# Summing the modulation vectors over partitions: two plain float32 matmuls into partitions 0 and 32 instead of four split ones

## The chip, the cores and the metric

The kernel runs on one core of a Trainium2 chip. The metric is the device time of one execution in microseconds (us). Before the change it is 2858.25 us, the median of three runs (2858.05 to 2859.9).

## The reference

The program computes one inference step through two trunk layers for 640 tokens (128 context, 512 latent) of width 1024. What matters here is the modulation at the head of each layer:

```python
mod_ctx = jax.nn.silu(c_ctx)[None, :] @ w_mod[l] + b_mod[l]
mod_lat = jax.nn.silu(c) @ w_mod[l] + b_mod[l]
...
sh1, sc1, g1, sh2, sc2, g2 = jnp.split(mod[:, None, :], 6, axis=-1)
```

`w_mod[l]` is 1024 x 6144, so each layer makes two vectors (one for each of two conditioning vectors) of 6144 numbers. The rest of a layer is projections, attention, a bidirectional state-space scan, two convolutions and a feed-forward block, nearly all of it matrix products over the 640 tokens.

## The kernel before, in words

Every operation is first recorded (by the helper at line 178, which is why nearly every row of the profile has L178), then a list scheduler (`Flow.issue`) orders all operations of the five lanes (TensorE, ScalarE, VectorE, GpSimd and the DMA queue of SyncE) by modelled costs and issues them in that order. Where several operations of a lane are ready, a rank decides, by the class of the operation: on TensorE the modulation class "m" goes first and the main stream "f" last; on ScalarE and VectorE "m" goes last. Buffers are granted in the order in which they were asked for. The cost model takes 4 cycles a column at 2.4 GHz for a plain float32 matmul and one cycle a column for a float32r one.

The big products run as float32r matmuls: each operand is split in two parts, `hi` (a rounding cast on ScalarE) and `lo` (the rest, a subtraction on VectorE), and three matmuls make one product. A few small products (scan states, cumulative sums) are plain float32 matmuls. In the names of the rows, `pf` is the PSUM of the main stream, `p`, `pp` and `pq` that of the others, `wh` and `wl` are the two parts of the weights.

The modulation is computed in groups of 512 columns, `mod_gen(l, m)`. The first four groups of layer 0 take another path (`mod_T_first`). The other 20 go through `mod_gen`: groups 4 to 9 of layer 0 step by step between the operations of attention (class "d", buffer `mw`), and groups 10 and 11 of layer 0 and all twelve of layer 1 in the feed-forward stage of layer 0 (class "m"). In each, VectorE multiplies eight pieces of `w_mod` (128 rows each) by the column of silu(cond) that belongs to them and adds them up in two accumulators `acc[0]` and `acc[1]` (named `macc` in the rows, 128 x 512, one for each conditioning vector). What is left is a sum over the 128 partitions, and that is done on TensorE: both accumulators are split in `hi` and `lo`, and four float32r matmuls with a stationary tile `pick[:, cnd, :]` (128 x 2: one column of ones, one of zeros) accumulate into rows 0 and 1 of one PSUM tile. `mod_rows` adds the bias (two copies of the same row, loaded by one DMA) and stores both rows in `modrow` in DRAM by one DMA. `mod_T` and `gate_bc` read `modrow` later.

Of the kernel before, what the change touches and what calls it, by code (L numbers as in the profile page):

```python
# [18 lines left out]
P = 128  # L19
# [21 lines left out]
def _mask(dims, cache={}):  # L41
    """Bits of the free elements that an access pattern touches."""
    m = cache.get(dims)
    if m is None:
        m = 1
        for s, n in reversed(dims):
            if s == 0 or n == 1:
                continue
            if m == 1 and s == 1:
                m = (1 << n) - 1  # L50
            else:
                b = 0
                for i in range(n):
                    b |= m << (s * i)
                m = b
        cache[dims] = m
    return m
# [22 lines left out]
class Flow:  # L80
    """Records the program as operations on tiles, orders them with a list scheduler (dependences by the
    elements touched, buffers granted in the order in which they were asked for) and issues them in that order."""

# [258 lines left out]
def hybrid_step_kernel(  # L342
# [42 lines left out]
    def keep(shape, dt, tag):  # L385
        return flow.tile(kp, shape, dt, tag, nm(tag), 1)
# [20 lines left out]

# [1 line left out]
    cst = keep([P, 3 * P], F32, "cst")  # L409
# [5 lines left out]
    dve.memset(neghalf, -0.5)  # L415
    pick = keep([P, 2, 2], F32R, "pick")

    def emit_consts():
        maskf = t2((P, P))
        dma.dma_start(cst[:, P:3 * P], consts[:, P:3 * P])  # L420
        dma.dma_start(maskf, consts[:, 3 * P:4 * P])
        dve.tensor_copy(mask, maskf)
        dve.memset(pick.rearrange("p a b -> p (a b)").bitcast(F32), 0.0)
        for k in range(2):
            act.copy(pick[:, k, k:k + 1], ones[:, 0:1])

# [1 line left out]
    cT = keep([P, 2, 8], F32, "cT")  # L428
# [13 lines left out]

# [1 line left out]
    modrow, attn_s, x_s, bm_s, row_s, sz_s, tg_s, ga_s, pb_s, y_sc = [], [], [], [], [], [], [], [], [], []  # L444
# [12 lines left out]

# [1 line left out]
    def wraw(parts, wide):  # L459
# [41 lines left out]

    # token-major product: stationary tokens, moving weights of 512 columns
    def tok_major(units, xT, ks):
# [14 lines left out]

    # tokens in two parts: tiles 0 to 2 and tiles 3 and 4
    def part(i):  # L520
# [5 lines left out]

    # tokens that wait in DRAM: two quads of feature tiles, in pieces of four, tile after tile
    def tok_load(src, q0):
# [17 lines left out]

    # feature-major product: stationary weights of 128 columns, moving tokens
    def feat_half(unit, cw, o, hT, b):
# [23 lines left out]
    def norm_x(xh, xns, junk):  # L572
        """Both halves of a token tile over their root mean square."""
        ssp = sm(2)
        for n in range(2):
            act.activation(junk, xh[n], AF.Square, accum_out=ssp[:, n:n + 1])
        ss = sm(1)
        pool.tensor_add(ss, ssp[:, 0:1], ssp[:, 1:2])
        rstd_of(ss, 1, 1.0 / DM)
        for n in range(2):  # L580
            dve.tensor_scalar(xns[n], xh[n], ss, None, ALU.mult)
# [20 lines left out]
    def norm_tile(x0, x1, t, i, modT, hT):  # L602
        """x0 and t are written over."""
        xns = [x0, t]
        norm_x([x0, x1], xns, t)
        for n in range(2):
            h = xns[n].rearrange("p (k t) -> p k t", k=4)
            norm_mod(norm_T(xns[n]), h, i, n, modT, hT, n == 0)

# [1 line left out]
    def mod_rows(l, m, ps, br):  # L611
        dve.tensor_add(br[0:2, :], ps[0:2, :], br[0:2, :])
        dma.dma_start(modrow[l][:, m * 512:(m + 1) * 512], br[0:2, :])

    def mw():
        """Of its own while attention holds the other buffers."""
        return t2() if flow.cls == "m" else flow.tile(tmp, [P, 512], F32, "mw", nm("mw"), 1)

    def mod_bias(l, m):
        br = mw()  # L620
        dma.dma_start(br[0:2, :], bc(b_mod[l:l + 1, m * 512:(m + 1) * 512], [2, 512]))
        return br

    def mod_gen(l, m):
        acc = [flow.tile(tmp, [P, 512], F32, "macc", nm("macc"), 2) for _ in range(2)]
        for kt in range(8):
            w = mw()
            dma.dma_start(w, w_mod[l, kt * P:(kt + 1) * P, m * 512:(m + 1) * 512])
            for cnd in range(2):
                s = cT[:, cnd, kt:kt + 1]  # L630
                if kt == 0:
                    dve.tensor_scalar(acc[cnd], w, s, None, ALU.mult)
                else:
                    dve.scalar_tensor_tensor(acc[cnd], w, s, acc[cnd], ALU.mult, ALU.add)
            yield
        ps = ps1()
        for cnd in range(2):
            hi, lo = t2(dt=F32R), t2(dt=F32R)
            split(hi, lo, acc[cnd])
            mm(ps[0:2, :], pick[:, cnd, :], hi, cnd == 0, False)  # L640
            mm(ps[0:2, :], pick[:, cnd, :], lo, False, cnd == 1)
        mod_rows(l, m, ps, mod_bias(l, m))
        yield
# [7 lines left out]

    # the first shifts and scales, straight to features on partitions: columns of silu(cond) in two parts
    def mod_T_first(ws):
# [3 lines left out]
        for n in range(2):  # L657
            for m in range(2):
                us = ws[4 * n + 2 * m:4 * n + 2 * m + 2]
                ps = psf()  # L660
                for kt in range(8):
                    for r in range(2):
                        w = us[kt // 4][r][:, (kt % 4) * 512:(kt % 4) * 512 + 512]
                        mm(ps[0:4, :], cs[:, kt].rearrange("p r a -> p (r a)"), w, kt + r == 0, kt + r == 8)
                flow.cls = "d"
                rows = t2() if n else flow.tile(tmp, [P, 512], F32, "macc", nm("macc"), 2)
                flow.cls = "f"
                o = m * 1024 + n * 512
                dma.dma_start(rows[4:6, :], bc(b_mod[0:1, o:o + 512], [2, 512]))
                act.copy(rows[0:4, :], ps[0:4, :])  # L670
                pt = flow.tile(p1, [P, 512], F32, "p1", nm("p1"), 2)
                for k in range(4):
                    pe.transpose(pt[:, 6 * k:6 * k + 6], rows[0:6, k * P:(k + 1) * P], ident[0:6, 0:6])
                # the two parts and the bias
                tv = t[:, :, 8 * m + 4 * n:8 * m + 4 * n + 4]
                dve.tensor_reduce(tv, pt[:, 0:24].rearrange("p (k r a) -> p a k r", k=4, r=3), AX.X, ALU.add)
                if m == 1:
                    dve.tensor_scalar(tv, tv, 1.0, None, ALU.add)
            yield t
# [23 lines left out]

# [1 line left out]
    def conv_bufs():  # L705
# [21 lines left out]
    def later(fn):  # L727
        """Record what was put off last, put this off in its stead."""
        old = list(pending)
        pending[:] = [fn]  # L730
        for f in old:
            f()
# [6 lines left out]

    # ================= the program as a list of items =================  # L740
    items = []
# [58 lines left out]
    def layer(l):  # L800
# [13 lines left out]
        def qk_normed(ps, n0, nh, t, a):  # L814
            """RMS norm per head, then rotary (t >= 1) or plain weights (t == 0); token-major."""
            src = ps[:, n0:n0 + nh * P]
# [83 lines left out]
        def attn_gen(g):  # L900
            kT, V = S["kT"], S["V"]
            qT, qc = S["qT", g], S["qc", g]
            # context tokens
            s = ps1()
# [53 lines left out]

# [1 line left out]
        def dt_item(ws):  # L960
# [71 lines left out]

# [1 line left out]
        def to_tok(cc, dst):  # L1034
            """feature-major padded [128, 642] -> token-major [128 tok, 5, 128 feat]"""
            for c0, n in ((0, 3), (3, 2)):
# [44 lines left out]

# [1 line left out]
        def z_item(g):  # L1083
# [21 lines left out]

# [1 line left out]
        def ssd_gen(g):  # L1107
# [19 lines left out]
            for c in range(NT):  # L1127
                o = col(c)
                dst = pb[:, 0:P] if c == 0 else pa[:, (c - 1) * P:c * P]
                mm(dst, Bf[:, o:o + P], Cf[:, o:o + P], True, True)  # L1130
            # C over B, and B by tokens behind it, in two parts
            s = slice(0, COLS)
# [21 lines left out]

            # context states leave as they are
            x = x_chunk(0)
# [227 lines left out]

# [1 line left out]
        def run_gen(key, make, n):  # L1386
# [127 lines left out]

# [1 line left out]
    AHEAD = 2  # L1516
# [68 lines left out]
```

## Time and profile before

| | |
|---|---|
| median of three runs | 2858.25 us |
| span of the profiled execution | 2854.8 us, 41191 instructions |
| own time of the profiled execution | not listed apart; the three runs lie 3.25 to 5.1 us above its span |
| TensorE (PE) busy | 2816.5 us, 99%, 15620 matmul records |
| VectorE (DVE) busy | 2066.4 us, 72% |
| ScalarE (ACT) busy | 1291.9 us, 45% |
| GpSimd (POOL) busy | 90.5 us, 3% |
| granted TensorE clock | 0.998 of 2.4 GHz |
| DMA | 478.45 MB, mean 168 GB/s |

A busy share is that of an engine over the whole span. A matmul record lasts from its issue to the end of its results, longer than the time that it holds the array: in a stream, the distance from one start to the next is what a matmul costs. `PEld` is the load of the stationary tile, which mostly runs under the matmul before it.

### The profile page before, as it was taken

To read this page: it belongs to the slowest core of one execution; us is meant where nothing else is said; L and a number is where in the kernel's file an instruction comes from. 1 tells how busy PE (TensorE), PEld (TensorE's weight loads), DVE (VectorE), ACT (ScalarE), POOL (GpSimd) and SP (SyncE) were. 2 spreads that over 40 slices of the span, in tenths; PEclk is the share of its full clock that TensorE was granted. 3 is DMA by queue.
4 is the path that set the end of the run, shared out by engine and by line. 5 is a ranking of instruction groups with operands and counts; after the bars stand their busy time and mean duration, and the time that the engine had idled before them with its cause. 6 is when DMAs were issued, how large, how long until landed. Compare 5 with 4: busy or idle time off the path is not lost.

```text
span 2854.8 us, 41191 instructions
## 1 busy us (share of the span) xinstructions
PE 2816.5 (99%) x15620; PEld 2456.6 (86%) x15620; DVE 2066.4 (72%) x2851; ACT 1291.9 (45%) x2255; POOL 90.5 (3%) x408
## 2 busy tenths in 40 slices
PE   6999999999999999999999999999999999999999
PEld 4898997877788898998979989887887888989898
DVE  7878775987799599997677666598779456545554
ACT  6454654445353453452444645544454325524342
POOL 1200000000000000000011000000000000000000
PEclk9999999999999999999999999999999999999999
DMA  7343444677868546455352223457667553252423
GB/s 262 100 125 126 126 151 143 225 247 245 275 219 275 180 136 215 167 175 180 98 168 85 94 95 100 155 199 251 220 235 258 203 175 132 86 166 65 155 84 111
DMA packets 309679, 478.45 MB, mean 168 GB/s; under 512 B 19808, under 2 KB 139792, under 8 KB 304360
## 3 DMA queue, kind: packets, MB, share of 16 engines
q1 hardware_dynamic: 309480, 475.81, 50.0%
q8 instruction: 123, 2.02, 0.3%
q14 instruction: 76, 0.62, 0.1%
HBM read 384.08 MB, written 91.65 MB: 167 GB/s over the span
## 4 chain that ended last, share of the span: by engine, by line
PE 95%; DMA 3%; DVE 1%; ACT 1%; issue 0%; SPq 0%; POOL 0%; DVEq 0%; ACTq 0%
PE pf L178 79%; PE p L178 10%; PE pp L178 4%; PE pq L178 1%; DMA tmp<-in_state_ssd_dram 1%; DMA slab<-in_w_mod_dram 0%; DVE tmp L178 0%; DMA ga<-tmp 0%; DVE wl L178 0%; DMA tmp<-in_x_prompt_dram 0%; ACT tmp L178 0%; SPq L178 0%; DMA slab<-in_q_norm_dram 0%; DVE slab L178 0%; ACT wh L178 0%
## 5 line engine op out<-in xcount | busy, mean ns | idle before, releaser
L178 PE MATMUL pf<-wh,slab 128*128 128x512 f32 x3920 | 1268.3, 400 | 5.9 <-ACT slab L178 2.5
L178 PE MATMUL pf<-slab,wh 128*128 128x256 f32 (+1 forms) x4416 | 980.2, 311 | 3.4 <-DVE slab L178 1.9
L178 PEld LDWEIGHTS pf<-wh,slab 128*128 128x128 f32 x3920 | 733.1, 189 | 174.4 <-issue 7.3
L178 PE MATMUL pf<-wl,slab 128*128 128x512 f32 x1960 | 780.7, 398 | 0.0
L178 PEld LDWEIGHTS pf<-slab,wh 128*128 128x128 f32 x4416 | 741.8, 189 | 12.0 <-issue 5.7
L178 PE MATMUL pf<-slab,wl 128*128 128x256 f32 (+1 forms) x2208 | 685.1, 310 | 0.0
L178 DVE TENSOR_TENSOR wl<-wr,wh 128x2048 fp32r<-128x2048 f32 (+1 forms) x156 | 350.7, 2248 | 145.3 <-ACT wh L178 144.5
L178 PEld LDWEIGHTS pf<-wl,slab 128*128 128x128 f32 x1960 | 369.5, 189 | 86.6 <-issue 6.0
L178 ACT CAST wh<-wr 128x2048 fp32r<-128x2048 f32 (+1 forms) x156 | 293.0, 1879 | 320.7 <-PE pf L178 302.4
L178 PEld LDWEIGHTS pf<-slab,wl 128*128 128x128 f32 x2208 | 415.9, 188 | 3.0 <-issue 0.2
L178 DVE SCALAR_TENSOR_TENSOR tmp<-tmp,fw,tmp 128x642 f32<-128x642 f32 x176 | 155.5, 885 | 80.5 <-ACT tmp L178 66.3
L178 PE MATMUL p<-tmp,slab 128*128 128x64 f32 (+1 forms) x976 | 209.8, 336 | 0.3 <-DVE tmp L178 0.3
L178 ACT ACTIVATE tmp<-tmp 128x642 f32<-128x642 f32 (+2 forms) x176 | 120.9, 687 | 179.1 <-DVE tmp L178 145.5
L178 ACT ACTIVATE tmp<-pf,fw 128x386 f32<-128x386 f32 (+1 forms) x176 | 109.0, 620 | 175.4 <-PE pf L178 172.2
L178 DVE TENSOR_TENSOR tmp<-pf,tmp 128x512 f32<-128x512 f32 x100 | 68.3, 688 | 132.1 <-PE pf L178 131.8
L178 PEld LDWEIGHTS p<-tmp,slab 128*128 128x128 f32 x976 | 136.0, 190 | 16.2 <-ACT tmp L178 4.6
L178 ACT COPY tmp<-pf 128x256 f32<-128x256 f32 (+3 forms) x296 | 127.5, 431 | 44.1 <-PE pf L178 43.7
L178 DVE TENSOR_TENSOR slab<-tmp,slab 128x512 fp32r<-128x512 f32 (+4 forms) x182 | 109.0, 634 | 42.9 <-ACT slab L178 42.7
L178 DVE SCALAR_TENSOR_TENSOR macc<-tmp,cT,macc 128x512 f32<-128x512 f32 x196 | 137.7, 743 | 1.2 <-DMA tmp<-in_w_mod_dram 1.2
L178 DVE TENSOR_TENSOR tmp<-tmp,tmp 128x512 f32<-128x512 f32 (+3 forms) x190 | 133.7, 705 | 3.0 <-DMA tmp<-sz 0.6
L178 PEld LDWEIGHTS p<-cst,tmp 128*128 128x128 f32 (+2 forms) x750 | 92.3, 141 | 40.6 <-issue 16.1
L178 PE MATMUL p<-cst,tmp 128*128 128x128 f32 (+2 forms) x750 | 121.0, 276 | 5.1 <-DMA tmp<-in_state_ssd_dram 4.4
(131 smaller groups left out, 2564.3 us busy)
## 6 DMA issues: line engine op xcount, KB each, us to landing
wr<-in_w_in_dram SPq DMA_DIRECT2D x60, 1024.0 KB
wr<-in_w_up_dram SPq DMA_DIRECT2D x44, 1024.0 KB
slab<-row SPq DMA_DIRECT2D x40, 1024.0 KB
tmp<-in_w_mod_dram SPq DMA_DIRECT2D x116, 256.0 KB
tmp<-xres SPq DMA_DIRECT2D x85, 256.0 KB
wr<-in_w_down_dram SPq DMA_DIRECT2D x20, 1024.0 KB
tmp<-xs SPq DMA_DIRECT2D x72, 256.0 KB
xres<-tmp SPq DMA_DIRECT2D x70, 256.0 KB
```

The source lines that it names most:

```text
L178: self.ops.append((lane, lambda: call(*args, **kw), self._cost(lane, fn, outs, ins, kw), deps, touched, self.cls))
```

## The change

The four float32r matmuls of a group become two plain float32 matmuls, each with a stationary column of ones, `ones[:, 0:1]`, and the accumulator itself as the moving tile. The first writes partition 0 of the PSUM tile, the second partition 32. The splitting of the accumulators (two casts on ScalarE, two subtractions on VectorE, four buffers) goes, and so does the tile `pick` with its memset and two casts. The bias is loaded to partitions 0 and 32 by two DMAs, added by two VectorE instructions of one partition each, and the rows are stored by two DMAs. The diff also takes out comments and docstrings, which record no operations.

```diff
@@
-    pick = keep([P, 2, 2], F32R, "pick")
...
-        dve.memset(pick.rearrange("p a b -> p (a b)").bitcast(F32), 0.0)
-        for k in range(2):
-            act.copy(pick[:, k, k:k + 1], ones[:, 0:1])
...
     def mod_rows(l, m, ps, br):
-        dve.tensor_add(br[0:2, :], ps[0:2, :], br[0:2, :])
-        dma.dma_start(modrow[l][:, m * 512:(m + 1) * 512], br[0:2, :])
+        for cnd in range(2):
+            r = slice(32 * cnd, 32 * cnd + 1)
+            dve.tensor_add(br[r, :], ps[r, :], br[r, :])
+            dma.dma_start(modrow[l][cnd:cnd + 1, m * 512:(m + 1) * 512], br[r, :])
...
     def mod_bias(l, m):
         br = mw()
-        dma.dma_start(br[0:2, :], bc(b_mod[l:l + 1, m * 512:(m + 1) * 512], [2, 512]))
+        for cnd in range(2):
+            dma.dma_start(br[32 * cnd:32 * cnd + 1, :], b_mod[l:l + 1, m * 512:(m + 1) * 512])
         return br
...
         ps = ps1()
         for cnd in range(2):
-            hi, lo = t2(dt=F32R), t2(dt=F32R)
-            split(hi, lo, acc[cnd])
-            mm(ps[0:2, :], pick[:, cnd, :], hi, cnd == 0, False)
-            mm(ps[0:2, :], pick[:, cnd, :], lo, False, cnd == 1)
+            mm(ps[32 * cnd:32 * cnd + 1, :], ones[:, 0:1], acc[cnd], True, True)
         mod_rows(l, m, ps, mod_bias(l, m))
```

## Rows read from the trace of the kernel before

**Rows 1.** The page: busy time of TensorE, and the chain that ended last.

```profile
PE 2816.5 (99%) x15620; PEld 2456.6 (86%) x15620; DVE 2066.4 (72%) x2851; ACT 1291.9 (45%) x2255; POOL 90.5 (3%) x408
...
PE 95%; DMA 3%; DVE 1%; ACT 1%; issue 0%; SPq 0%; POOL 0%; DVEq 0%; ACTq 0%
```

**Rows 2.** Busy time by stretches: us, engines, granted clock, DMA share, GB/s.

```profile
860.00:1345.00 485.00, 483.30 (x2729) 431.14 (x2728) 416.36 (x565) 190.39 (x297) 11.77 (x91) 1.00 0.58 193
130.00:440.00 310.00, 309.69 (x1953) 286.37 (x1952) 238.79 (x351) 168.20 (x313) 9.44 (x50) 1.00 0.41 127
```

**Rows 3.** Matmul groups by shape: stationary, moving, records, busy us, mean ns, idle before.

```profile
L178 PE MATMUL p<-tmp,pick 128*2 128x512 f32 x80 | 28.3, 395 | 0.0
...
L178 PE MATMUL p<-cst,tmp 128*64 128x256 f32 x20 | 5.8, 397 | 0.6 <-ACT tmp L178 0.6
L178 PE MATMUL p<-tmp,tmp 128*128 128x512 f32 x8 | 4.1, 592 | 0.0
...
L178 PE MATMUL p<-tmp,ones 128*128 128x320 f32 x4 | 1.4, 432 | 0.0
```

**Rows 4.** Timeline of TensorE: start, length, what, around a group's four matmuls.

```profile
1336.55 0.63 PE L178 MATMUL p<-tmp,pick 128*2 128x512 f32 x2
1337.02 0.41 PE L178 MATMUL pf<-slab,wh 128*128 128x256 f32 x2
...
1337.60 0.40 PE L178 MATMUL p<-tmp,pick 128*2 128x512 f32 x1
1337.84 0.28 PE L178 MATMUL pf<-slab,wl 128*128 128x256 f32 x1
```

**Rows 5.** Timeline of TensorE: a plain float32 matmul of 320 columns.

```profile
467.86 0.70 PE L178 MATMUL p<-tmp,ones 128*128 128x320 f32 x2
```

**Rows 6.** Timeline of TensorE: a plain float32 matmul with 64 stationary columns.

```profile
1827.96 0.62 PE L178 MATMUL pf<-wh,slab 128*128 128x512 f32 x2
1828.51 0.19 PEld L178 LDWEIGHTS p<-cst,tmp 128*64 128x64 f32 x2 [0.36 <-ACT et L178]
1828.51 0.65 PE L178 MATMUL p<-cst,tmp 128*64 128x256 f32 x2
1829.09 0.19 PEld L178 LDWEIGHTS pf<-wl,slab 128*128 128x128 f32 x1 [0.39 <-issue]
1829.09 0.50 PE L178 MATMUL pf<-wl,slab 128*128 128x512 f32 x1
...
1829.43 0.63 PE L178 MATMUL pf<-wh,slab 128*128 128x512 f32 x2
```

**Rows 7.** Timeline of TensorE: two such matmuls in a row (four records).

```profile
473.66 0.63 PE L178 MATMUL pf<-wh,slab 128*128 128x512 f32 x2
474.22 0.62 PEld L178 LDWEIGHTS p<-cst,tmp 128*64 128x64 f32 x4 [0.36 <-issue]
...
475.56 0.63 PE L178 MATMUL pf<-wh,slab 128*128 128x512 f32 x2
```

**Rows 8.** Timeline of VectorE: last accumulations of two modulation groups.

```profile
1136.26 3.40 DVE L178 SCALAR_TENSOR_TENSOR macc<-tmp,cT,macc 128x512 f32<-128x512 f32 x5
...
1215.47 1.41 DVE L178 SCALAR_TENSOR_TENSOR macc<-tmp,cT,macc 128x512 f32<-128x512 f32 x2
...
1220.27 0.74 DVE L178 SCALAR_TENSOR_TENSOR macc<-tmp,cT,macc 128x512 f32<-128x512 f32 x1
```

**Rows 9.** Groups of VectorE: the splits and the bias addition.

```profile
L178 DVE TENSOR_TENSOR tmp<-macc,tmp 128x512 fp32r<-128x512 f32 x40 | 27.0, 686 | 2.5 <-ACT tmp L178 1.2 <-PE p L178 1.0
...
L178 DVE TENSOR_TENSOR tmp<-p,tmp 2x512 f32<-2x512 f32 x14 | 9.4, 674 | 1.9 <-PE p L178 1.9
```

**Rows 10.** Group of ScalarE: the casts of the accumulators.

```profile
L178 ACT CAST tmp<-macc 128x512 fp32r<-128x512 f32 x40 | 24.6, 625 | 16.1 <-DMA tmp<-xres 8.6 <-DVE macc L178 7.4
```

**Rows 11.** Instructions of one tile: an issue of a bias load on SyncE's queue.

```profile
L178 SPq DMA_DIRECT2D macc<-in_b_mod_dram x2: 252/252/253, 20.1 to 22.6; - x2
```

**Rows 12.** Waits of TensorE: for whom, us in total, times, longest.

```profile
PE p L178 <- DMA tmp<-in_state_ssd_dram: 4.4, 5, 1.4
...
PE pq L178 <- DMA tmp<-modrow: 2.4, 1, 2.4
```

## The prediction

> **What bounds the kernel now.** I read the page first. TensorE is busy 99% of the span and carries 95% of the chain that ended last [rows 1]. Then I read the stretches in which the 20 groups of `mod_gen` send their matmuls (from 154 to 436 us and from 993 to 1338 us): of the 310 us from 130 to 440 TensorE is idle for 0.3 us, and of the 485 us from 860 to 1345 for 1.7 us; the granted clock is 1.00 in both, so TensorE runs at its upper level of 2.4 GHz [rows 2]. So each microsecond of TensorE that the change adds there goes into the end time, and work taken off ScalarE or VectorE can give back no more than those 2.0 us of idle time. The groups of matmuls by shape show what is affected [rows 3], and the timeline what each of them really costs, from start to start [rows 4 to 7].
>
> **The matmuls that go.** There are 80 of them, four in each of 20 groups [rows 3]. Each lasts 0.395 us, but that is not its price. Two from 1336.55 and the next of the main stream at 1337.02 make 0.235 us for one, and 1337.60 to 1337.84 gives 0.24 [rows 4]; the pair's length of 0.63 less one record of 0.395 gives 0.235 too. I take 0.23, the distance of the main stream's own matmuls of 512 columns (0.62 less 0.395 is 0.225 [rows 6]). Removed: 80 x 0.23 = 18.4 us.
>
> **The matmuls that come.** A plain float32 matmul is two records here: `ones` is multiplied once in each of two layers and has four records [rows 3]. The two records of one such matmul of 320 columns last 0.70 us together and 0.432 each, so the second starts 0.27 us after the first [rows 5, 3]. That is 320 columns at two cycles of 2.4 GHz each, 0.267 us. The record of 512 columns is longer than that of 320 by 0.592 - 0.432 = 0.160 us for 192 more columns, again two cycles a column [rows 3]. So one pass of 512 columns takes 512 x 2 / 2.4 GHz = 0.427 us, and a matmul two of them; the single stationary column saves nothing of this, since the time goes with the moving columns. Added: 20 x 2 x 2 x 0.427 = 34.1 us. The exchange alone is +15.7 us.
>
> **The switch in and out.** No matmul of before has a single stationary column in plain float32 or writes at partition 32. The nearest is the one with 64 stationary columns of plain float32, and it has a cost that no other shape in the trace has: its weight load starts only when the array is empty, and so does the load of the matmul behind it ("0.36" and "0.39" idle of the weight loads) [rows 6]. In numbers: the two matmuls from 1827.96 hold the array until 1828.42 (2 x 0.23). The main stream is back on the array 0.23 us before the start at 1829.43, that is at 1829.20. Of these 0.78 us two passes of 256 columns take 0.427, and 0.35 us are lost. With two such matmuls in a row the array is away from 473.66 + 0.46 = 474.12 to 475.56 - 0.23 = 475.33, 1.21 us, of which four passes take 0.853 [rows 7]: 0.36 us lost, so the price is for one excursion, not for a matmul. The two-column float32r matmuls that go pay nothing like it (0.235 each, above). The bounds for a single column are 0 (it pays as the `pick` matmuls do) and 0.36 (as with 64 columns); it is plain float32 and narrow, so I take the nearest row, 0.35.
>
> The Trainium skill (TensorEngine Tiling (Array Packing), Key Properties) says that a change of the tiling mode drains TensorE while a change of tile within a mode does not. Its list of modes has a tile of 128 x 32, which is what one stationary column would use; by that rule the drain holds here as in the 64-column rows, and partitions 0 and 32 in a row are one excursion, as I take it.
>
> How many excursions? One for a group if both matmuls stand together in TensorE's order, two if main-stream matmuls come between. The first matmul can go when `acc[0]` is done, the second when `acc[1]` is. The first takes 0.853 us, and VectorE finishes one accumulation 0.66 us after another when they are adjacent (five in 3.40 us, 0.745 each), so the second is ready in time then; where another operation of VectorE lies between, it is not. From the timeline of VectorE I went through the last two accumulations of all 20 groups: adjacent in 8 (as at 1136.26), apart in 12 (as 1215.47 and 1220.27) [rows 8]. So 8 + 2 x 12 = 32 excursions, 11.2 us at 0.35; the bounds are 20 (7.0) and 40 (14.0), as the scheduler will order anew.
>
> **What lies beside.** 40 casts of 0.625 us leave ScalarE, 40 subtractions of 0.686 us leave VectorE, and VectorE gets 20 additions of 0.67 us more (the addition's time goes with its 512 columns, not with its partitions) [rows 9, 10]. TensorE's waits name no such operation in any size [rows 12], so this counts as nothing; at most it gives back the 2.0 us of idle time. Four buffers fewer are asked for in each group, under the same cover. The queue of SyncE gets 40 small DMAs more, at 0.25 us an issue [rows 11]. The second store waits for the second addition, so each of 20 stores may hold the loads queued behind it for some 0.7 us; who would wait is the weight stream, and through it TensorE, up to 14 us in all. The weights are prepared two items ahead, TensorE waits for DMAs only for states and `modrow` [rows 12], and the wait for states is for data that the change does not touch. I take nothing. The memset and two casts of `pick` cost TensorE nothing either.
>
> The list scheduler will order everything behind the first group anew. TensorE has little idle time to gain; what a new order loses I put at up to 4 us either way, an estimate from the idle time in [rows 2] and the few us in [rows 12].
>
> **The sum.** -18.4 + 34.1 + 11.2 = +26.9 us. It is made against the profiled execution's span of 2854.8 us, which gives 2881.7; its own total time is not listed, but the median lies 3.45 us above that span, and with that the time is 2858.25 + 26.9 = **2885 us** (+0.9%).
>
> **The rivals.**
> - *Overlap of the two column groups.* The second matmul's first pass writes another part of the array than the first matmul's second pass, so they could run at once. The passes are issued in order (two of the first, then two of the second), so only one of four can be hidden: 0.427 us for each group whose matmuls stand together. With 8 of them the sum is 26.9 - 3.4 = +23.5, 2882 us; with all 20 together it is 15.7 + 7.0 - 8.5 = +14.2, 2872 us. No two tiles of one mode at different partitions occur in the trace, so it speaks neither for nor against. The four passes of [rows 7] ran one after another, but at one place.
>  The Trainium skill (the same page and section) says that tiles work independently and in parallel, which is this rival.
> - *No drain with one column.* If the matmul is handled as those of `pick` were, only the exchange remains: +15.7, 2874 us. For it: their stationary tile is as narrow and they pay nothing. Against it: they are float32r, and the plain float32 matmul with a narrow tile pays each time.
> - *Not slower.* Both matmuls of a group run wholly side by side and the switch hides under the streams around it: 20 x 0.853 = 17.1 us for 18.4, -1.3 us, and with the 2.0 us of idle time returned 2855 us. A pair together costs 1.71 + 0.35 = 2.06 us for 0.92 removed, so it decides from the point where 1.14 us of a pair are hidden. Against it: issue in order, and 12 of 20 groups with their halves apart.
> - *One pass only.* Were a one-column matmul done in one pass at one cycle a column, it would be 40 x 0.23 = 9.2 for 18.4, with the drains +2.0, 2860 us. Against it: every plain float32 product in [rows 3] has two records at two cycles.
> - *The new order or the SyncE queue costs.* Up to 14 us of held loads, or all groups apart (40 excursions): 2888 to 2899 us.
>
> **How the numbers follow.** The forecast has a chance of 0.48, its own range being 2880 to 2890 (20 to 40 excursions, the order's 4 us in part). Overlap 0.25, no drain 0.08, not slower 0.04, one pass 0.02, the dear order 0.13. The range of 2871 to 2892 takes the forecast, overlap and no drain, and leaves out the rest, less than 2 in 10. A measurement of this kernel can tell about 0.2% (5.7 us) from no change: faster by more than that 0.03, within it 0.05, slower 0.92.
>
> **What would show it.** In the profile after: 80 records of `p<-macc,ones`, 128*1 by 512, each some 0.59 us long; TensorE's busy time longer by 15 us or more with its idle time as before; weight loads with 0.3 to 0.4 us of idle time in front, at the entry and the exit of each excursion, about 32 of them; the casts and subtractions of `macc` gone; ScalarE and VectorE less busy by 25 and 14 us with no gain. The distance from the last stream before a pair to the first behind it says 2.06 us (serial) or 1.63 (overlap). It is wrong if a pair's records overlap by more than their tails, if the loads behind them start at once, or if the growth lies after 1345 us, where no such matmul is.

## The result and the profile after

The median of the runs with the change is 2879.65 us (2878.93 to 2880.73), that of the kernel before, measured beside it, 2859.07 us: 20.6 us more. The ratio on record is 1.0077, with a 95% interval of 1.0064 to 1.0089, so the change costs between 18.3 and 25.4 us. That is slower, as forecast, and 5 us under the forecast of 2885. The profiled execution's span grew from 2854.8 to 2878.9 us.

The page of the kernel after, TensorE and the chain that ended last, against [rows 1]:

```profile
PE 2839.1 (99%) x15620; PEld 2449.9 (85%) x15620; DVE 2058.2 (71%) x2830; ACT 1269.9 (44%) x2213; POOL 91.9 (3%) x408
...
PE 92%; DMA 4%; DVE 2%; ACT 1%; issue 1%; SPq 1%; POOL 0%; DVEq 0%; ACTq 0%
```

TensorE is busy 22.6 us longer. ScalarE has 22.0 us less to do and VectorE 8.2 us less, and the end time shows nothing of either. The stretches of [rows 2], in the same columns (us, engines in the order PE, PEld, DVE, ACT, POOL, granted clock, DMA share, GB/s):

```profile
130.00:440.00 310.00, 309.34 (x1925) 279.79 (x1924) 231.81 (x342) 157.95 (x297) 11.32 (x52) 1.00 0.41 126
860.00:1345.00 485.00, 482.90 (x2626) 411.30 (x2625) 405.63 (x550) 173.72 (x271) 12.57 (x85) 1.00 0.59 190
```

TensorE is idle for 0.7 and 2.1 us there, against 0.3 and 1.7 before, at the same granted clock. So the time is not in a new wait. The stretches are equally full, but the same work of the main stream ends later. The groups by shape (busy us, mean ns, idle before) show what is new:

```profile
L178 PE MATMUL p<-macc,ones 128*1 128x512 f32 x80 | 36.4, 591 | 0.5 <-DVE macc L178 0.2
...
L178 DVE TENSOR_TENSOR tmp<-p,tmp 1x512 f32<-1x512 f32 x28 | 19.1, 681 | 9.7 <-PE p L178 9.3
...
L178 DVE TENSOR_TENSOR mw<-p,mw 1x512 f32<-1x512 f32 x12 | 8.1, 678 | 3.6 <-DMA mw<-in_b_mod_dram 2.4 <-PE p L178 1.1
```

There are 80 records, as before, but of plain float32 and 591 ns each, as long as the nearest shape in [rows 3]; and an addition of one partition takes as long as one of two [rows 9]. What such a matmul costs TensorE's stream is read from the timeline (start, length, engine, line, what; in brackets the idle time in front and what ended it). The first five lines are around a matmul that stands alone, the next five around two that stand together, then come a group whose second matmul waits for the addition to the first's row, and one whose second accumulator is late:

```profile
1130.50 0.63 PE L178 MATMUL pf<-wh,slab 128*128 128x512 f32 x2
1131.06 0.09 PEld L178 LDWEIGHTS p<-macc,ones 128*1 128x1 f32 x2 [0.37 <-DVE tmp L178]
1131.06 1.02 PE L178 MATMUL p<-macc,ones 128*1 128x512 f32 x2
1132.01 0.19 PEld L178 LDWEIGHTS pf<-wl,slab 128*128 128x128 f32 x1 [0.86 <-issue]
1132.35 0.63 PE L178 MATMUL pf<-wh,slab 128*128 128x512 f32 x2
...
441.00 0.39 PE L178 MATMUL pf<-wh,slab 128*128 128x512 f32 x1
441.32 0.09 PEld L178 LDWEIGHTS p<-macc,ones 128*1 128x1 f32 x4 [0.36 <-issue]
441.32 1.03 PE L178 MATMUL p<-macc,ones 128*1 128x512 f32 x4
442.27 0.19 PEld L178 LDWEIGHTS pf<-wh,slab 128*128 128x128 f32 x1 [0.86 <-issue]
442.61 0.40 PE L178 MATMUL pf<-wl,slab 128*128 128x512 f32 x1
...
148.68 1.02 PE L178 MATMUL p<-macc,ones 128*1 128x512 f32 x2
149.73 0.68 DVE L178 TENSOR_TENSOR mw<-p,mw 1x512 f32<-1x512 f32 x1
150.47 0.09 PEld L178 LDWEIGHTS p<-macc,ones 128*1 128x1 f32 x2 [0.55 <-DVE mw L178]
...
1170.54 1.38 PE L178 MATMUL p<-macc,ones 128*1 128x512 f32 x4
1170.90 0.09 PEld L178 LDWEIGHTS p<-macc,ones 128*1 128x1 f32 x2 [0.27 <-DVE macc L178]
```

The price is the time in which the array is not with the main stream. Alone: the main stream's two matmuls hold it until 1130.50 + 0.46 = 1130.96, and it is back 0.23 us before the start at 1132.35, that is at 1132.12: 1.16 us. Together: from 441.23 to 442.38, 1.15 us for *both* matmuls. Two records last 1.02 us and four last 1.03.

In this way I went through all groups of both kernels. Before, the 80 matmuls cost 18.8 us. After, there are 35 excursions: 30 with one matmul (median 1.148 us) and 5 with both, three of these at 1.15 and two, with a late accumulator, near 1.5 (an excursion is one trip of TensorE from the main stream into these matmuls and back). Together they cost 41.6 us. The difference of +22.8 us lies within the measured interval. (The two passes of a matmul take 0.853 us, so 0.295 us of an excursion go to the switch.) Where the growth lies, layer 1's `p<-tmp,ones` matmul shows: the tile's last record starts at 1851.0 us, and before it started at 1827.2, so 23.8 of the span's 24.1 us have come by then. Its first record, behind the six groups in attention, starts at 475.0 us and started at 467.9.

### The profile page after: what moved, and what is told of

Same layout as the page of the kernel before. It is cut to its first block, busy times and chain, and to the rows that moved or that the text cites. A ratio compares the mean times of both kernels' runs of the same rounds, so it can differ in the third digit from the quotient of the medians.

```text
span 2878.9 us, 41156 instructions
## 1 busy us (share of the span) xinstructions
PE 2839.1 (99%) x15620; PEld 2449.9 (85%) x15620; DVE 2058.2 (71%) x2830; ACT 1269.9 (44%) x2213; POOL 91.9 (3%) x408
## 4 chain that ended last, share of the span: by engine, by line
PE 92%; DMA 4%; DVE 2%; ACT 1%; issue 1%; SPq 1%; POOL 0%; DVEq 0%; ACTq 0%
PE pf L178 76%; PE p L178 10%; PE pp L178 3%; PE pq L178 1%; DMA slab<-row 1%; DVE tmp L178 1%; DMA tmp<-xs 1%; DMA tmp<-in_state_ssd_dram 1%; SPq L178 1%; DVE slab L178 0%; DMA slab<-in_w_mod_dram 0%; DMA tmp<-modrow 0%; DVE wl L178 0%; ACT tmp L178 0%; DMA tmp<-in_x_prompt_dram 0%
## 5 line engine op out<-in xcount | busy, mean ns | idle before, releaser
L178 PEld LDWEIGHTS p<-tmp,slab 128*128 128x128 f32 x976 | 136.2, 190 | 18.3 <-issue 5.3
L178 DVE TENSOR_TENSOR tmp<-p,tmp 128x512 fp32r<-128x512 f32 (+1 forms) x108 | 74.1, 687 | 79.3 <-ACT tmp L178 69.3
```

The lines of the kernel that those rows point to most:

```text
L178: self.ops.append((lane, lambda: call(*args, **kw), self._cost(lane, fn, outs, ins, kw), deps, touched, self.cls))
```

## The experiments

All ratios are to the kernel before on the same chip, where its median lay between 2857.9 and 2858.9 us; the us behind a ratio are its share of that median, and a "price" is the sum over all 20 groups, taken as above, less the 18.8 us of before. By a column group I mean the PSUM partition (0, 32, 64 or 96) from which a narrow matmul writes. Theory A of the expectations is that the loss is TensorE's time in the excursions, 1.15 us each whether one matmul or two column groups are in it. The rivals have the other letters. In this kernel the list scheduler orders everything behind an edited operation anew, so most edits change two things, their own and the order, and the later runs try to part them.

**e1: both matmuls together.** The first matmul also waits for the second accumulator (`flow.ops[-1][3]` is the set of operations for which the one recorded last waits).

```diff
+            done = len(flow.ops) - 1
             yield
...
             mm(ps[32 * cnd:32 * cnd + 1, :], ones[:, 0:1], acc[cnd], True, True)
+            flow.ops[-1][3].add(done)
```

> The changed kernel with one more dependence: the first of a group's two matmuls waits for both accumulators, so that both stand next to each other in TensorE's order in all 20 groups (5 of 20 in the changed kernel). Theory A (plain float32 passes of 0.43 us, 0.31 us for an excursion into the narrow tile, both column groups wholly side by side when they stand together, 15 groups apart): 1.15 us a group for 0.92 before, 20 x 0.23 = +4.6 us, about 2863.5. Theory B (the growth is the new order of the rest, the extra DMAs and additions): it stays near +20 us, 2879. Theory C (the passes of two column groups run one after another; the short pairs in the trace are an artefact of modelled ends): 20 x (1.71 + 0.31 - 0.92) = +22 us, 2881.

Measured: 1.0030 [1.0018, 1.0041], +8.6 us. Waiting makes the kernel 12 us faster than the change as it stands. The rivals' +20 falls. The price is +8.5 us: nearly all groups cost 1.15 us with four records in them, but one costs 1.79 and one 3.43, and one group is still apart. That is the 4 us by which A's +4.6 was too low. A late accumulator in the timeline of this kernel:

```profile
1149.44 1.68 PE L178 MATMUL p<-macc,ones 128*1 128x512 f32 x4 [1.55 <-DVE macc L178]
```

**e2: both in one column group.** On the kernel before: plain float32, `pick` in float32, both matmuls into partitions 0 and 1, together.

```diff
-    pick = keep([P, 2, 2], F32R, "pick")
+    pick = keep([P, 2, 2], F32, "pick")
...
-            mm(ps[0:2, :], pick[:, cnd, :], hi, cnd == 0, False)
-            mm(ps[0:2, :], pick[:, cnd, :], lo, False, cnd == 1)
+            mm(ps[0:2, :], pick[:, cnd, :], acc[cnd], cnd == 0, cnd == 1)
+            flow.ops[-1][3].add(done)
```

> The kernel before with its four split matmuls replaced by two plain float32 ones that accumulate into rows 0 and 1 of one column group (stationary tile 128 x 2, one column of ones), forced to stand together; one bias load, one addition, one store as before. Theory A: no overlap in one column group, 4 passes of 0.427 and 0.31 for the excursion, 2.02 us a group for 0.92: +22 us, about 2881. If overlap does not need two partitions: +4.6 us, 2863.5. Theory B (the extra DMAs and additions cost): near 2859, since they are not in it.

Measured: 1.0068 [1.0051, 1.0085], +19.4 us; price +21.6, or 2.0 us a group. The timeline around one group:

```profile
1313.87 0.40 PE L178 MATMUL pf<-wh,slab 128*128 128x512 f32 x1
1314.20 0.09 PEld L178 LDWEIGHTS p<-macc,pick 128*2 128x2 f32 x2 [0.36 <-issue]
1314.20 1.88 PE L178 MATMUL p<-macc,pick 128*2 128x512 f32 x4
1316.01 0.19 PEld L178 LDWEIGHTS pf<-wh,slab 128*128 128x128 f32 x1 [0.86 <-issue]
1316.35 0.39 PE L178 MATMUL pf<-wl,slab 128*128 128x512 f32 x1
```

Four records last 1.88 us in one place, and 1.03 us in two. This pair of runs shows the overlap, and that it is whole: partition 32 is worth 0.85 us a pair, two of four passes. In e2 both matmuls also add into the same rows, but that is not what sets them one behind the other: the two of [rows 7] write different PSUM tiles at the same partitions, with nothing added up, and their four passes ran one after the other too.

**e3: both always apart.** The second matmul waits for the addition to the first's row; the bias is loaded first.

```diff
+        br = mod_bias(l, m)
...
+            if cnd:
+                flow.ops[-1][3].add(first)
+            first = mod_row(l, m, ps, br, cnd)
```

> The changed kernel with one more dependence: the second matmul of a group waits for the addition of the first one's row, so that all 20 groups are apart (15 of 20 in the changed kernel). Theory A: two excursions of 1.16 us for 0.92 in each group, 20 x 1.40 = +28 us, about 2887. Theories B and C: an excursion apart costs what it costs together, so no more than the changed kernel, 2880 plus or minus 3.

Measured: 1.0156 [1.0141, 1.0171], +44.6 us. The price is +27.1, from 40 excursions of 1.148, as A has it. But 17 us more are lost elsewhere, which A did not expect; most of it is one long stop. Here the timeline of TensorE at its end:

```profile
897.43 1.22 PE L178 MATMUL pf<-wh,slab 128*128 128x512 f32 x2 [11.53 <-DVE tmp L178]
```

The stretch around it and two parts of it, columns as in the first such table:

```profile
880.00:900.00 20.00, 8.47 (x34) 6.29 (x32) 17.16 (x29) 3.07 (x6) 1.37 (x2) 0.76 0.87 280
890.50:897.43 6.93, 0.00 (x1) 0.01 (x1) 6.93 (x12) 0.62 (x1) 0.00 (x0) 0.50 0.83 249
897.43:900.70 3.27, 3.26 (x8) 2.15 (x9) 2.94 (x5) 0.00 (x0) 0.00 (x0) 0.50 1.01 380
```

And the chain of waits that leads to it (start, length, what):

```profile
878.31 2.02 DMA y<-tmp
881.20 4.20 DMA tmp<-y
885.42 0.63 ACT slab L178
...
888.14 0.81 DVE macc L178 x2
896.77 0.61 DVE tmp L178
```

Where one stage follows the other, the last `y` tile is stored, loaded again and split, and VectorE runs modulation sums in between; TensorE stands for 11.5 us. The granted clock falls to the lower of its two levels (1.2 GHz) within the stop and stays there for 10.2 us, 3.3 of them behind the stop, hence the mean of 0.76.

**e4: a wide stationary tile.** 65 columns, zeros but for one column of ones, so both matmuls use the whole array.

```diff
+    sel = keep([P, 97], F32, "sel")
+    dve.memset(sel, 0.0)
+    dve.memset(sel[:, 32:33], 1.0)
...
-            mm(ps[32 * cnd:32 * cnd + 1, :], ones[:, 0:1], acc[cnd], True, True)
+            mm(ps[0:65, :], sel[:, 32 - 32 * cnd:97 - 32 * cnd], acc[cnd], cnd == 0, cnd == 1)
```

> The changed kernel with a stationary tile of 65 columns (one of ones, the rest zeros) for each matmul, both accumulating into one PSUM tile, so that rows 0 and 32 come out as before but the whole array is used: plain float32 without the narrow tile. Theory A: no empty array at entry and exit and no overlap, 1.71 us a group for 0.92: 20 x 0.79 = +15.8 us, about 2875, and weight loads that run under the matmul before. If plain float32 itself empties the array: 0.31 for each excursion on top, 2881 to 2887. Theory B: as the changed kernel, 2879.

Measured: 1.0061 [1.0042, 1.0081], +17.4 us; price +17.7. The timeline:

```profile
1317.93 0.39 PE L178 MATMUL pf<-wl,slab 128*128 128x512 f32 x1
1317.94 0.36 PEld L178 LDWEIGHTS p<-macc,sel 128*65 128x65 f32 x2
1318.16 1.88 PE L178 MATMUL p<-macc,sel 128*65 128x512 f32 x4
1319.48 1.03 PE L178 MATMUL pf<-wh,slab 128*128 128x512 f32 x2
1320.35 0.39 PE L178 MATMUL pf<-wl,slab 128*128 128x512 f32 x1
```

The time alone does not tell A's +15.8 from the +20 of theory B; the timeline does. The weight load no longer waits: it runs under the matmul before it. The array is away from 1318.16 to 1320.35 - 0.46 = 1319.89 us, 0.86 us a matmul, which is its two passes and nothing more. So plain float32 alone does not cost the 0.295 us. Nor does a narrow stationary tile alone: the float32r matmuls of before have two columns and cost 0.235 us each. It takes both.

**e5 and e6: all four column groups.** If two column groups run side by side, four should too. e5 splits each row in halves of 256 columns (on e1); e6 takes two modulation groups of the feed-forward stage at once with four accumulators (the six groups in attention go as in e5).

```diff
-        for cnd in range(2):
-            mm(ps[32 * cnd:32 * cnd + 1, :], ones[:, 0:1], acc[cnd], True, True)
+        for n in range(4):
+            mm(ps[32 * n:32 * n + 1, 0:256], ones[:, 0:1], acc[n // 2][:, n % 2 * 256:n % 2 * 256 + 256], True, True)
```

```diff
+    def mod_pair(l, m):
+        acc = [flow.tile(tmp, [P, 512], F32, "macc", nm("macc"), 2) for _ in range(2)] + [t2(), t2()]
...
+        for n in range(4):
+            mm(ps[32 * n:32 * n + 1, :], ones[:, 0:1], acc[n], True, True)
+            flow.ops[-1][3].add(done)
```

> As the run with both matmuls together, but each accumulator's 512 columns are summed in two halves of 256, four matmuls of 256 columns into partitions 0, 32, 64 and 96, all waiting for both accumulators. Theory A (one excursion of 0.31 us, all column groups side by side): two passes of 0.213 and 0.31 make 0.74 us a group where the kernel before needs 0.94 (four of 0.235): 20 x -0.20 = -4 us, about 2855, less whatever a late accumulator costs. If only two column groups run side by side: 1.17 us a group, +4.6 us. Theory C (one after another): 2.0 us a group, +22 us.

> As the run with halves for the six groups in attention; the 14 groups of the feed-forward stage go in seven pairs, four accumulators of 512 columns each into partitions 0, 32, 64 and 96 at once. Theory A: 1.15 us for a pair for 1.88 before, 7 x -0.73 = -5.1 us, and 6 x -0.20 = -1.2 us: -6.3 us, about 2852.5, if no accumulator is late. Theory C: +22 us.

Measured: 1.0078 [1.0066, 1.0091] and 1.0077 [1.0064, 1.0091], both about +22 us. Both expectations missed: the time is what theory C says, but the trace is not. The groups that go without a wait cost what A says (0.74 us in e5, 1.16 a pair in e6), but they are few: in e5 eleven groups cost 1.8 to 2.0 us and four 2.9, in e6 five of the seven pairs 3.4 to 5.1. One of e5's at 1.8 in the timeline:

```profile
1277.98 0.60 PE L178 MATMUL p<-macc,ones 128*1 128x256 f32 x4
1278.63 0.41 DVE L178 TENSOR_TENSOR tmp<-p,tmp 1x256 f32<-1x256 f32 x1 [0.80 <-PE p L178]
1279.09 0.09 PEld L178 LDWEIGHTS p<-macc,ones 128*1 128x1 f32 x4 [1.02 <-DVE tmp L178]
1279.10 0.60 PE L178 MATMUL p<-macc,ones 128*1 128x256 f32 x4 [0.51 <-DVE tmp L178]
```

Two matmuls go, the scheduler puts an addition behind them, and the other two wait for it, as it reads the same PSUM tile at another partition. The wait stands inside the excursion, so TensorE has nothing else to do.

**e7: the beside work alone.** The matmuls of before, with two bias loads, two additions of half the columns and two stores a group.

```diff
-        dve.tensor_add(br[0:2, :], ps[0:2, :], br[0:2, :])
-        dma.dma_start(modrow[l][:, m * 512:(m + 1) * 512], br[0:2, :])
+        for h in range(2):
+            c = slice(256 * h, 256 * h + 256)
+            dve.tensor_add(br[0:2, c], ps[0:2, c], br[0:2, c])
+        for cnd in range(2):
+            dma.dma_start(modrow[l][cnd:cnd + 1, m * 512:(m + 1) * 512], br[cnd:cnd + 1, :])
```

> The kernel before with its own four split matmuls, but two bias loads, two additions (of 256 columns each, both rows) and two stores for each group, as many as the changed kernel has. Theory A: none of this reaches TensorE, 0 us (2856 to 2862 with a new order). Theory B (they are the cost): +10 us or more.

Measured: 1.0044 [1.0031, 1.0057], +12.6 us, where A expected nothing. The `pick` matmuls cost 18.8 us as before; the loss is the wait of e3, in TensorE's waits between 860 and 1345 us (us in total, times, longest):

```profile
PE pf L178 <- DVE tmp L178: 10.1, 1, 10.1
```

The lower clock comes with it here too (first within the stop, then behind it):

```profile
883.20:890.80 7.60, 0.08 (x1) 0.08 (x1) 7.60 (x13) 0.62 (x1) 0.00 (x0) 0.50 0.93 316
890.80:896.90 6.10, 6.10 (x17) 4.79 (x18) 6.10 (x11) 1.20 (x2) 0.00 (x0) 0.50 0.87 276
```

Whether the added instructions or the new order bring this wait, e7 leaves open.

**e10: the same beside work in the order of before.** An operation keeps its place in the plan and issues two instructions in place of one (`flow.instead` replaces what the operation recorded last issues).

```diff
         dve.tensor_add(br[0:2, :], ps[0:2, :], br[0:2, :])
+        flow.instead(lambda: (add(0), add(1)))
         dma.dma_start(modrow[l][:, s], br[0:2, :])
+        flow.instead(lambda: (store(0), store(1)))
```

> The kernel before in exactly its own order of operations; each bias load and each store is issued as two, each addition as two of 256 columns, in the place of the one. The run with doubled rows and a new order was 14 us slower, with a wait of 10.1 us of TensorE at 878 us and 13.7 us at half clock behind it. If the new order was its cause: 0 plus or minus 1.5 us, about 2858.5. If the extra DMAs and additions are: +14 us again.

Measured: 1.0006 [0.9998, 1.0015], not to be told from no change. The 60 instructions more cost at most 4 us, and nothing that can be measured; the wait of e7 is its order.

**e8 and e9: e5 and e6 with every addition behind the last matmul.** The wait inside the excursion is to go, and the scheduler is told the matmul's cost (185 ns in e8; in e9 also 288 ns for the 512 columns). `flow.last` gives the operation recorded last one more operation to wait for, and a cost.

```diff
-            flow.ops[-1][3].add(done)
+            flow.last(done, 185.0)
+        end = len(flow.ops) - 1
...
             dve.tensor_add(br[r, 0:256], ps[r, 0:256], br[r, 0:256])
+            flow.last(end)
```

> As the run with halves, but the four additions wait for the last of a group's four matmuls, and the scheduler is told 0.185 us for each of these matmuls (0.74 for a group). In the run with halves the second half of the matmuls waited for additions that read the same PSUM bank: 1.84 us a group in 9 groups, 2.9 in 4, and 0.74 in 5 without such a wait. Theory A: 0.74 us for 0.94 in every group, -4 us, about 2855. If the four column groups do not run side by side, or the additions were not the cause: +15 us or more.

> As the run with pairs of groups, additions after the last matmul, and the scheduler told 0.288 us for each matmul of 512 columns (1.15 for a pair) and 0.185 for each of 256. Theory A: -6.3 us, about 2852.5. Otherwise +10 us or more, as without it.

Measured: 1.0104 [1.0087, 1.0122] and 1.0099 [1.0081, 1.0116], +30 and +28 us, in which both expectations fail. The prices are near what A has, -1.1 us in e8 (0.72 to 0.78 in 16 groups, two of the other four in two excursions and one at 2.0) and -3.8 in e9 (1.15 to 1.18 in six of the seven pairs, 2.15 in one). But both meet the wait of e3 and e7 at the change of stage, 12.2 and 10.7 us long; e8's TensorE is idle 27 us longer than before in all, and works 15 us longer at the lower clock (27 us for 12), half of which is lost. In e9 price and added idle time (17 us) make some 13 of the 22 us by which its profiled run was longer, and 14 us more of work at the lower clock (26 us for 12) some 7 of the rest.

**e11 and e12: e5's and e1's matmuls in the order of before.** The casts, subtractions and split matmuls issue nothing; at the place of the last subtraction the plain matmuls are issued, four of 256 columns in e11, two of 512 in e12 (by `both`).

```diff
+            act.copy(hi, acc[cnd])
+            flow.instead(lambda: None)
+            dve.tensor_sub(lo, acc[cnd], hi.bitcast(F32))
+            flow.instead(both if cnd else lambda: None)
             mm(ps[0:2, :], pick[:, cnd, :], hi, cnd == 0, False)
+            flow.instead(lambda: None)
```

> The order that the scheduler made for the kernel before, kept for all else: casts, subtractions and the four split matmuls of a group issue nothing, and in the place of its last subtraction stand four plain float32 matmuls of 256 columns, ones against the halves of both accumulators, into partitions 0, 32, 64 and 96; bias loads, additions and stores are issued as four in the place of one. No stall at the change of stages at about 880 us can come from a new order. Theory A: 0.74 us for 0.94 in each of 20 groups, -4 us, about 2855 (if it waits nowhere for an accumulator). If the new orders were not what cost the earlier runs with halves: +20 us or more.

> The same with the two matmuls of the changed kernel (512 columns, partitions 0 and 32) next to each other in the place of the last subtraction, two bias loads, additions and stores. Theory A: 1.15 us for 0.94, 20 x 0.21 = +4.2 us, about 2863; the rest of the changed kernel's 20.6 us is then from standing apart. If the plain matmuls cost 20 us however they stand: 2879.

Measured: 1.0038 [1.0023, 1.0053], +10.9 us, and 1.0052 [1.0036, 1.0068], +14.9 us. Both are some 11 to 15 us above A's totals (-4 and +4.2). The prices are now near what A says in every group: -4.0 us in e11 (0.72 to 0.77 each) and +4.3 in e12 (1.14 to 1.19 each). One group of e11 in the timeline of TensorE:

```profile
1344.75 0.10 PEld L659 LDWEIGHTS p<-macc,ones 128*1 128x1 f32 x8
1344.75 0.61 PE L659 MATMUL p<-macc,ones 128*1 128x256 f32 x8
1345.29 0.30 PEld L183 LDWEIGHTS pf<-slab,wh 128*128 128x128 f32 x2 [0.44 <-issue]
```

And of TensorE's waits in e11 the one that is new:

```profile
PE p L183 <- ACT tmp L183: 9.0, 6, 2.0
```

Eight records last 0.61 us, as long as four of 256 columns in e5: all four column groups ran side by side. The timelines of TensorE and VectorE in e12 show where such waits come from, the matmuls of a group and the additions to its rows 119 us later:

```profile
889.38 1.03 PE L655 MATMUL p<-macc,ones 128*1 128x512 f32 x4
...
1008.51 2.81 DVE L622 TENSOR_TENSOR tmp<-p,tmp 1x512 f32<-1x512 f32 x4
```

TensorE's wait in e12, between 860 and 1345 us:

```profile
PE p L183 <- ACT tmp L183: 8.4, 5, 2.0
```

From 889 to 1008 us the group holds one of the two PSUM tiles that the rows call `p`, and the transposes of the norms, which want both, go through one. In the kernel before no `pick` matmul of this stretch runs ahead of 993.7 us, so the tile is taken later there. That this is the cause is read from the timelines; no run moved the additions alone. Price and waits make 12.7 of e12's 14.9 us, and 5.0 of e11's 10.9; some 6 us of e11 stay open.

## Why the prediction was right, and where its terms were off

- **The bound.** Right. TensorE's own time is the loss: 22.6 us more of busy time, 0.8 us more of idle time in the two stretches, and nothing of the 30 us taken off ScalarE and VectorE comes back. e10 and the page of the profile agree on that.
- **The matmuls that go.** 18.8 us measured for 18.4.
- **Two passes of 0.427 us.** Right: e4 has 0.86 us a matmul with no switch in it.
- **The switch.** Right in kind, large by a sixth: 0.295 us for one stationary column, where 0.35 was taken from the 64 columns of [rows 6]. With e4 and [rows 4] it is shown that it comes with plain float32 in a narrow tile, and with neither alone. This agrees with the Trainium skill (TensorEngine Tiling (Array Packing), Key Properties), by which a change of mode drains TensorE. The sign "0.3 to 0.4 us" in front of the exit's weight load was too small: it is 0.86 us, as the load stands behind the passes.
- **How many excursions.** 35 for 32. The count of adjacent accumulations (8) said when the second matmul could go, but only 5 groups stayed together. In 7 of the other 15 the addition to the first row, which reads the PSUM tile that the second matmul writes, ran in front of that matmul; in 6 of these the trace names it as what the second weight load waited for last, as at 150.47 us above. In the other 8 the second accumulator was finished only 0.8 to 3.2 us after the first matmul had started. TensorE did other work meanwhile, so a group apart cost a second excursion and some 0.3 us of waiting at most.
- **The step that failed** is "issued in order (two of the first, then two of the second), so only one of four can be hidden", and with it the serial pair of 2.06 us in the likeliest case. The two matmuls of a pair run wholly side by side: 1.15 us together (after, e1, e12), 2.0 us in one column group (e2). The prediction's own sign of being wrong, a pair's records that overlap by more than their tails, came true: four last 1.03 us where two last 1.02. The sentence of the Trainium skill (TensorEngine Tiling (Array Packing), Key Properties) that tiles work independently, which stood there as the rival's, agrees with this; the argument from the order of issue was mine and no row bore it. That it came out small is luck: only 5 of 20 groups were together. 2879.65 us lies just under the forecast's own 2880 to 2890 and nearer to the rival's 2882. Had the change sent all 20 together, the prediction's terms for that case (15.7 + 7.0 = +22.7) would have missed e1's +8.6 by 14 us.
- **What lies beside.** Nothing, as said, for the instructions themselves (e10). The term "up to 4 us either way" for a new order was right for this kernel but far too narrow as a bound: in e3, e7, e8 and e9 a new order cost a wait of 10 to 12 us at one place.

The terms set beside each other: passes 35 x 0.853 = 29.9 for 34.1 (-4.3), switches 10.3 for 11.2 (-0.9), waits inside excursions +1.4 for 0, removed 18.8 for 18.4 (-0.4). So 26.9 becomes 22.7.

What decides whether an order meets the wait at 880 us isn't settled. In the four kernels that meet it layer 0's attention ends late (its first `ones` matmul at 481.6 to 496.2 us, against 462 to 475.5 in before, after, e1, e2 and e4 to e6), but no run changed that alone. No version here was faster than the kernel before. The summing matmuls of e11 take 4.0 us less of TensorE than the split ones, but no order was found that gives this back; a version that adds e11's rows early within before's order wasn't tried.

## What to carry to other kernels

Price a small matmul from the end of the main stream in front of it to its return behind it, since a mean duration hides both the overlap and the switch. A narrow plain float32 matmul costs a switch for each trip of the stream, not for each matmul, so collect those for different column groups into one trip, and keep readers of their PSUM tile behind the last of them. Before blaming an edit for a time under a list scheduler, put the edit into the old order: here the same 60 instructions cost 12.6 us in a new one and nothing in the old.

## What the runs showed of the hardware

- Plain float32 matmuls into different column groups run side by side though they stand one behind the other: 1.15 us for one or two of 512 columns (0.853 us of passes), 0.74 us for four of 256 (0.427 us of passes). Two into one column group take 2.0 us (e2).
- The switch costs 0.295 us a trip with one stationary column, and nothing with 65 (e4) or with the two float32r columns of before (0.235 us a matmul).
- In a stop of TensorE of 10 to 11.5 us the granted clock fell to 1.2 GHz before the stop ended and stayed there for 3.3 us (e3) and 6.1 us (e7) of the work behind it.
